# Gates and two key products taken up column by column, and a tile of w_in loaded among the modulation's tiles

## The chip, the core and the metric

One core of a Trainium2 chip runs the whole program. The metric is the device time of one execution in microseconds; of the kernel before, three runs are shown, and their median counts. The engines are TensorE (PE; its weight loads are listed apart as PEld), VectorE (DVE), ScalarE (ACT), GpSimd (POOL) and SyncE (SP), which here issues nearly all DMA transfers. Each engine works through a queue of its own in order, and waits on semaphores for the others.

## The reference

Two transformer blocks run on 256 tokens of 1024 features, in float32. Only the head of the first block matters here:

```python
mod = jnp.matmul(c_act, w_ada[l]) + b_ada[l]
sh_m, sc_m, gt_m, sh_f, sc_f, gt_f = jnp.split(mod, N_MOD, axis=-1)
h = modulate(rmsnorm(x, norm_mix_g[l]), sh_m, sc_m)
proj = jnp.matmul(h, w_in[l])
q, k, v, f_logit, u = jnp.split(proj, split_pts, axis=-1)
log_f = jax.nn.log_sigmoid(f_logit.astype(jnp.float32) + b_fgate[l].astype(jnp.float32))
attn_out = forgetting_attention(q, k, v, log_f)
```

`c_act` is one vector, silu(c), so `mod` is a vector of 6 x 1024. Attention, a pooling branch, a mixture of 32 experts (read whole, 96 MB) and a second block follow. `lb` is a bound of the second block's forget gates, a softmax over two rows of 512 numbers.

## The kernel before

**Stream.** Weights come in tiles of 128 x 2048 numbers (1 MB). `Stream.add` lists them in the order of the string `plan` (line 183) with the slot of a ring that each takes; `a` stands for the modulation's tiles of shift and scale of the first half (8), `b` and `c` for its other two groups, `i` for w_in (8), `o` for w_out (4). SP issues the loads in that order, each when its slot is free and when the load eight places ahead of it has landed. `next()` gives a whole tile. `next2()` gives half a tile of w_in split into an upper part `whi` (line 70, ACT) and a lower part `wlo` (line 71, DVE), with up to two halves split ahead; there are three buffers of each.

**Modulation.** `ada_first` (line 280 on) handles tile d of group a, which holds what column d (features 128 d to 128 d + 127) needs of shift and scale: eight matmuls with the vector `cs` as weights (line 292, 32 rows each), a copy to SBUF by ACT (`mr`, line 294), two matmuls with ones that sum over the partitions (line 298), an addition of the bias into `modT` (line 299). The products of column d + 1 are issued ahead of the sums of column d. Then `A1` (line 359) and `evac_split` (lines 337 to 353) make column d of the modulated input out of the transposed x: an upper part `hT`, a lower part `hL`. Even columns use DVE, ACT, POOL in turn; odd columns ACT, DVE, DVE.

**Products.** `mmx` (lines 140 to 142) takes three matmuls for one product of split operands: upper x upper, upper x lower, lower x upper. When all eight columns stand, PE computes the forget gate `pf` (24 matmuls with 8 columns of weights), then the four key products by `feat` (24 matmuls and a copy to `kT`, line 395, each), the values, and then queries and pooling inputs. The gate's tail (lines 377 to 390: ACT functions, a scan on DVE, a three-way split into `F3`) is needed by the first attention scores. Between products, `some()` takes up a tile of groups b or c: four matmuls on PE (line 311), an accumulation on DVE (lines 313, 315).

**Start.** ACT and DVE make `cs` from c, then `lb` and `olb` (lines 226 to 232), then the row statistics of x (`rms_scale`) and the scaled `xn` (lines 257, 259); PE transposes `xn` in 16 steps (`transposed`, line 274) ahead of everything else.

Of the kernel before, what the change touches and what calls it, by code (L numbers as in the profile page):

```python
# [9 lines left out]
F32 = mybir.dt.float32  # L10
# [4 lines left out]
OP = mybir.AluOpType  # L15
# [8 lines left out]
def nb(tag):  # L24
    return {"f3": 3, "t5": 5}.get(tag, 4)
# [97 lines left out]
def body(tc, nc, ctx, a, out):  # L123
# [56 lines left out]
    st.slots.update({i: (ring if i < 4 else ring2, f"w{i}") for i in range(11)})  # L180

    st.slots.update({15: (hp_, "hT"), 16: (hp_, "hL")})
    plan = "a0-7 0-7 i0-4 0-4 b0-3 5-8 i5 9 b4 10 b5 5 i6 6 b6-7 7-8 c0 0 i7 1 c1-2 2-3 o0 8 c3 10 c4 5 c5 7 o1 0 c6 4 c7 2 o2 3 o3 10"
    src = {"a": (a["w_ada"][0], 0), "b": (a["w_ada"][1], 0), "c": (a["w_ada"][2], 0), "i": (a["w_in"], 1), "o": (a["w_out"], 1)}

    def span(x):
# [31 lines left out]
    G.memset(cs, 0.0)  # L218
    V.tensor_tensor(cs[:, :, 0], cT, ce, op=OP.mult)


    lbl = vec[:, V_LB:V_LB + 8].rearrange("p (r h) -> p r h", r=2)
    lb = cp.tile([128, 4], F32, name="lb")
    olb = cp.tile([128, 4], F32, name="olb")
    le_ = q1.tile([128, 2, 4], F32, name="le_")
    V.tensor_tensor(lb, lbl[:, 0], lbl[:, 1], op=OP.max)
    V.tensor_tensor(le_, lbl, lb[:, None, :].to_broadcast([128, 2, 4]), op=OP.subtract)
    S.activation(le_, le_, AF.Exp)
    V.tensor_tensor(lb, le_[:, 0], le_[:, 1], op=OP.add)
# [34 lines left out]
    for t in range(2):
        scale_rows(xn, xt, r1, t)

    def transposed(ps, tag, src):
        r = []
        for c2 in range(4):
            pt = ps.tile([128, 2, 256], F32, name="ptr", tag=tag, bufs=nb(tag))  # L270
            for c in range(2):
                for t in range(2):
                    d = 2 * c2 + c
                    nc.tensor.transpose(pt[:, c, 128 * t:128 * t + 128], src[:, t, 128 * d:128 * d + 128], ident)
            r += [pt[:, 0], pt[:, 1]]
        return r

    xT = transposed(ps, "a", xn)


    modT = cp.tile([128, 6, 8], F32, name="modT")

    def ada_first():

        last = None
        for d in range(9):
            if d < 8:
                w = st.next()
                pa = ps.tile([128, 512], F32, name="pa", tag="m", bufs=2)
                for k in (0, 2, 4, 6, 1, 3, 5, 7):  # L290
                    j = 32 * (k // 2)
                    mm(pa[j:j + 32, 0:256], cs[:, k, :], w[:, 256 * k:256 * k + 256], start=(k % 2 == 0), stop=(k % 2 == 1))
                mr = q1.tile([128, 256], F32, name="mr", bufs=2)
                S.activation(mr, pa[:, 0:256], AF.Copy)
            if last:
                pl, ml = last
                for j in range(2):
                    mm(pl[:, 256 + j:257 + j], ml[:, 128 * j:128 * j + 128], ones, start=True, stop=True)
                V.tensor_tensor(modT[:, 0:2, d - 1], pl[:, 256:258], vec[:, V_BA + d - 1:V_BA + 16:8], op=OP.add)
                yield  # L300
            last = pa, mr
# [27 lines left out]
    def mod(m):  # L329
        return modT[:, m]  # L330
# [27 lines left out]
    for d, _ in enumerate(ada_first()):
        V.scalar_tensor_tensor(A1[:, d:d + 1], mod(1)[:, d:d + 1], 1.0, vec[:, V_GM + d:V_GM + d + 1], op0=OP.add, op1=OP.mult)
        evac_split(q1, xT[d], hT[:, d], hL[:, d], A1[:, d:d + 1], mod(0)[:, d:d + 1], v=d % 2)  # L360
    st.split_to(LOOK)
# [8 lines left out]
    G.memset(F3, 0.0)  # L370
    catH = q1.tile([128, 8, 256], F32R, name="catH")
    catL = q1.tile([128, 8, 256], F32R, name="catL")

    pf = ps.tile([128, 256], F32, name="pf", tag="a", bufs=4)
    for k in range(8):
        mmx(pf[0:8], (wfh[:, k], wfl[:, k]), (hT[:, k], hL[:, k]), start=(k == 0), stop=(k == 7))
    fz = q1.tile([8, 256], F32, name="fz", tag="mr", bufs=2)
    S.activation(fz, pf[0:8], AF.Identity, bias=vec[0:8, V_BF:V_BF + 1])
    fa = q1.tile([8, 256], F32, name="fa", tag="mr", bufs=2)
    S.activation(fa, fz, AF.Abs)  # L380
    S.activation(fa, fa, AF.Exp, scale=-1.0)
# [9 lines left out]
    def feat(w, dst, scale=1.0):
        p = ps.tile([128, 256], F32, name="pp", tag="a", bufs=4)
        for k in range(8):
            mmx(p, sub(w, slice(None), slice(128 * k, 128 * k + 128)), (hT[:, k], hL[:, k]), start=(k == 0), stop=(k == 7))
        S.activation(dst, p, AF.Copy, scale=scale)
# [1395 lines left out]
```

## Time and profile before

| what | value |
|---|---|
| median of three runs | 743.89 us (743.48 to 747.61) |
| the profiled execution, its own time | 744.4 us |
| its span in the trace | 742.8 us |
| PE busy | 677.4 us (91%) |
| DVE busy | 396.8 us (53%) |
| ACT busy | 303.5 us (41%) |
| DMA, first 350 us | about 420 GB/s, but for two dips |
| DMA, whole span | 207.70 MB, mean 280 GB/s |

Busy time of PE is modelled at its matmuls' ends, and matmuls overlap, so a busy PE is not a PE at its peak. Shares are means over stages with different limits; the prediction reads single stretches.

### The profile page before, as it was taken

How to read it: one execution, taken by the hardware profiler on the slowest of the kernel's cores; microseconds unless marked ns; L12 is line 12 of the kernel's file. 1: busy time of each engine (PE TensorE's matmuls, PEld its weight loads, DVE VectorE, ACT ScalarE, POOL GpSimd, SP SyncE). 2: the span in 40 equal slices, each digit the busy share in tenths (PEclk: the TensorE clock that was granted, in tenths of full speed). 3: DMA queues.
4: the chain of work that ended last, by engine and by line, in shares of the span. 5: the costliest groups of instructions: out<-in, count | busy, mean ns of one | idle time of the engine just before them, and what ended most of it. 6: DMA issues, size and time to landing. Idle time of an engine off the chain costs nothing.

```text
span 742.8 us, 12245 instructions
## 1 busy us (share of the span) xinstructions
PE 677.4 (91%) x4953; PEld 524.9 (71%) x4953; DVE 396.8 (53%) x664; ACT 303.5 (41%) x531; POOL 132.9 (18%) x134
## 2 busy tenths in 40 slices
PE   3899999889799777768999999999999999999995
PEld 2698867654244313132799999999989998989885
DVE  2676896522122102020888876877867654545545
ACT  3644534320011001000675566596456654535433
POOL 0103521000000000000204242212413530503201
PEclk9999999999979979898999999999999999999998
DMA  9999599989999999999764333355446556455411
GB/s 356 419 420 415 205 398 421 419 356 422 420 417 422 421 421 421 421 422 421 301 227 169 116 114 114 115 207 191 170 170 212 214 180 217 170 195 203 171 58 56
DMA packets 29726, 207.70 MB, mean 280 GB/s; under 512 B 3553, under 2 KB 3937, under 8 KB 4706
## 3 DMA queue, kind: packets, MB, share of 16 engines
q1 hardware_dynamic: 29520, 206.35, 70.8%
q8 instruction: 41, 0.67, 0.4%
q10 hardware_dynamic: 146, 0.53, 0.2%
q14 instruction: 19, 0.16, 0.1%
HBM read 205.81 MB, written 1.05 MB: 279 GB/s over the span
## 4 chain that ended last, share of the span: by engine, by line
PE 53%; DMA 15%; DVE 3%; issue 1%; ACT 1%; DVEq 0%; ACTq 0%; SPq 0%
DMA w<-in_w_gu 11%; PE pp L140 9%; PE pp L141 9%; PE pp L142 9%; DMA w<-in_w_dn 4%; PE fy L142 4%; PE fy L141 4%; PE fy L140 4%; PE pB L1274 2%; PE pg L810 2%; PE y L847 2%; PE pv L140 1%; PE pd L964 1%; PE pv L142 1%; PE pv L141 1%; PE acc L141 1%
## 5 line engine op out<-in xcount | busy, mean ns | idle before, releaser
L71 DVE TENSOR_TENSOR wlo<-w,whi 128x1024 fp32r<-128x1024 f32 x146 | 184.7, 1268 | 98.9 <-ACT whi L70 98.8
L70 ACT ACTIVATE whi<-w 128x1024 fp32r<-128x1024 f32 x146 | 153.3, 1054 | 78.3 <-PE fy L142 39.7
L140 PE MATMUL pp<-hT,whi 128*128 128x256 f32 x368 | 104.4, 284 | 0.0
L142 PE MATMUL pp<-hT,wlo 128*128 128x256 f32 x368 | 102.5, 279 | 0.5 <-DVE wlo L71 0.5
L141 PE MATMUL pp<-hL,whi 128*128 128x256 f32 x368 | 102.3, 278 | 0.0
L930 PE MATMUL pgu<-w,hg 128*32 128x512 f32 x512 | 67.7, 646 | 22.6 <-DMA w<-in_w_gu 22.5
L140 PEld LDWEIGHTS pp<-hT,whi 128*128 128x128 f32 x368 | 69.2, 188 | 3.4 <-issue 2.4
L140 PE MATMUL pp<-nH,whi 128*128 128x256 f32 x256 | 71.5, 279 | 0.0
L141 PE MATMUL pp<-nL,whi 128*128 128x256 f32 x256 | 71.3, 279 | 0.0
L142 PE MATMUL pp<-nH,wlo 128*128 128x256 f32 x256 | 71.3, 279 | 0.0
L142 PEld LDWEIGHTS pp<-hT,wlo 128*128 128x128 f32 x368 | 69.2, 188 | 0.8 <-DVE wlo L71 0.7
L141 PEld LDWEIGHTS pp<-hL,whi 128*128 128x128 f32 x368 | 69.4, 189 | 0.0
L930 PEld LDWEIGHTS pgu<-w,hg 128*32 128x32 f32 x512 | 14.2, 112 | 72.5 <-issue 46.3
L1553 POOL TENSOR_TENSOR aL<-rs,aH 128x256 fp32r<-128x256 f32 x32 | 46.2, 1445 | 86.6 <-ACT aH L1552 80.7
L934 DVE TENSOR_TENSOR act<-pgu,act 128x256 f32<-128x256 f32 x8 | 3.4, 424 | 105.3 <-ACT act L933 105.3
L933 ACT ACTIVATE act<-pgu 128x256 f32<-128x256 f32 x8 | 3.1, 384 | 128.2 <-PE pgu L930 128.2
L142 PEld LDWEIGHTS pp<-nH,wlo 128*128 128x128 f32 x256 | 48.6, 190 | 0.0
L141 PE MATMUL fy<-wlo,aH 128*128 128x512 f32 x124 | 48.2, 389 | 0.0
L140 PE MATMUL fy<-whi,aH 128*128 128x512 f32 x124 | 48.2, 389 | 0.0
L142 PE MATMUL fy<-whi,aL 128*128 128x512 f32 x124 | 48.2, 389 | 0.0
L141 PEld LDWEIGHTS pp<-nL,whi 128*128 128x128 f32 x256 | 48.1, 188 | 0.1
L140 PEld LDWEIGHTS pp<-nH,whi 128*128 128x128 f32 x256 | 48.1, 188 | 0.1
(428 smaller groups left out, 1276.1 us busy)
## 6 DMA issues: line engine op xcount, KB each, us to landing
w<-in_w_gu SPq DMA_DIRECT2D x64, 1024.0 KB, 19.6
w<-in_w_dn SPq DMA_DIRECT2D x32, 1024.0 KB, 19.6
w<-in_w_ff SPq DMA_DIRECT2D x32, 1024.0 KB, 4.8
w<-in_w_in SPq DMA_DIRECT2D x30, 1024.0 KB, 5.4
w<-in_w_ada SPq DMA_DIRECT2D x24, 1024.0 KB, 12.9
w<-in_w_out SPq DMA_DIRECT2D x8, 1024.0 KB, 4.7
w<-in_w_o SPq DMA_DIRECT2D x4, 1024.0 KB, 4.8
xt<-in_x SPq DMA_DIRECT2D x1, 1024.0 KB, 5.0
```

Of the source, the lines that this page charges most:

```text
L70: nc.scalar.activation(hi, w, AF.Copy)
L71: low = lambda e, lo=lo, w=w, hi=hi: e.tensor_tensor(lo, w, hi.bitcast(F32), op=OP.subtract)
L140: mm(out_, l[0], r[0], start=start, stop=False)
L141: mm(out_, l[0], r[1], start=False, stop=False)
L142: mm(out_, l[1], r[0], start=False, stop=stop)
L810: mm(pg[:, d], xn[:, t, 512 * b + 128 * d:512 * b + 128 * d + 128], Pf[:, t], start=(t == 0), stop=(t == 1))
L847: mm(pacc[t][h], pw[g][:, 128 * t:128 * t + 128], o, start=False, stop=(g == 7))
L930: mm(pgu[32 * j:32 * j + 32], hg[g][:, k, 32 * j:32 * j + 32], w[:, 512 * j:512 * j + 512], start=(k == 0), stop=(k == 7))
L934: V.tensor_tensor(act, pgu[:, 256:512], act, op=OP.mult)
L964: mm(pd[32 * j:32 * j + 32], aT[:, f, 32 * j:32 * j + 32], w[:, 512 * j:512 * j + 512], start=(f == 0), stop=(f == 1))
L1274: mm(p[:, 4 * t + h], kt[:, h, 128 * t:128 * t + 128], qo[:, h, n * t:n * t + n], start=True, stop=True)
L1553: G.tensor_tensor(aL[:, f], s, aH[:, f].bitcast(F32), op=OP.subtract)
```

## The change

Four things are done.

1. In `plan`, the first tile of w_in (i0) is loaded after four of the modulation's eight tiles, into slot 8 instead of slot 0; tile b3 goes to slot 0 instead of slot 8. The rest of the order stays.
2. `ada_first` is taken apart into `ada_products(d)` and `ada_sums(d)`; the latter also makes column d of `hT` and `hL`. The products of column 0 are issued ahead of the transposes, and the transposes, four at a time (`turned0`), between the first columns.
3. `column(i, ks, kinds)` issues the matmuls of the forget gate (i = 2) and of the first two key products (i = 0, 1) for given columns only. It is called between the modulation's steps, as far as columns stand. Both halves of i0 are split after the sums of column 3. The gate and kT[1] take their PSUM buffers from tag "s". The number of matmuls is as before.
4. kT[2] and kT[3] come next, and only then the gate's tail; `lb` and `olb` are moved from the start to behind the gate's tail.

```diff
-    plan = "a0-7 0-7 i0-4 0-4 b0-3 5-8 i5 9 b4 10 b5 5 i6 6 b6-7 7-8 c0 0 i7 1 c1-2 2-3 o0 8 c3 10 c4 5 c5 7 o1 0 c6 4 c7 2 o2 3 o3 10"
+    plan = "a0-3 0-3 i0 8 a4-7 4-7 i1-4 1-4 b0-2 5-7 b3 0 i5 9 b4 10 b5 5 i6 6 b6-7 7-8 c0 0 i7 1 c1-2 2-3 o0 8 c3 10 c4 5 c5 7 o1 0 c6 4 c7 2 o2 3 o3 10"
...
-    V.tensor_tensor(lb, lbl[:, 0], lbl[:, 1], op=OP.max)
-    V.tensor_tensor(le_, lbl, lb[:, None, :].to_broadcast([128, 2, 4]), op=OP.subtract)
-    S.activation(le_, le_, AF.Exp)
-    V.tensor_tensor(lb, le_[:, 0], le_[:, 1], op=OP.add)
-    V.reciprocal(lb, lb)
-    V.tensor_tensor(lb, lb, le_[:, 0], op=OP.mult)
-    V.tensor_scalar(olb, lb, -1.0, 1.0, op0=OP.mult, op1=OP.add)
...
+    def column(i, ks, kinds=((0, 0), (0, 1), (1, 0))):
+
+        if i == 2 and not pf:
+            pf.append(ps.tile([128, 256], F32, name="pf", tag="s", bufs=2))
+        if i < 2 and not early:
+            early.extend((ps.tile([128, 256], F32, name="pp", tag=tag, bufs=n), st.next2(False)) for tag, n in (("a", 4), ("s", 2)))
+        for m, n in kinds:
+            for k in ks:
+                o, w = (pf[0][0:8], (wfh, wfl)[m][:, k]) if i == 2 else (early[i][0], early[i][1][m][:, 128 * k:128 * k + 128])
+                c = begun[i] = begun.get(i, 0) + 1
+                mm(o, w, (hT, hL)[n][:, k], start=(c == 1), stop=(c == 24))
+
+    upper_, lower_ = ((0, 0), (0, 1)), ((1, 0),)
+    ada_products(0)
+    for t in range(2):
+        scale_rows(xn, xt, r1, t)
+    turned0(0)
+    ada_sums(0)
+    turned0(1)
+    ada_products(1)
+    turned0(2)
+    ada_sums(1)
+    turned0(3)
+    ada_products(2)
+    column(2, (0,))
+    ada_sums(2)
+    column(2, (1,))
+    ada_products(3)
+    ada_sums(3)
+    st.split_to(2)
+    column(2, (2,))
+    column(0, (0, 1, 2), upper_)
+    column(0, (0, 1, 2), lower_)
+    ada_products(4)
+    column(1, (0, 1, 2))
+    for d in range(4, 7):
+        ada_sums(d)
+        ada_products(d + 1)
+        if d < 6:
+            for i in range(3):
+                column(i, (d - 1,))
+    column(0, (5,))
+    column(1, (5,))
+    ada_sums(7)
+    st.split_to(1)
+    column(2, (5,))
+    for i in range(3):
+        column(i, (6,))
+    both = ((0, 0), (1, 0))
+    for i in range(3):
+        column(i, (7,), both)
+    for i in range(3):
+        column(i, (7,), ((0, 1),))
...
+    for i in range(2):
+        S.activation(kT[:, i], early[i][0], AF.Copy)
+    for i in range(2, 4):
+        feat(st.next2(), kT[:, i])
     fz = q1.tile([8, 256], F32, name="fz", tag="mr", bufs=2)
-    S.activation(fz, pf[0:8], AF.Identity, bias=vec[0:8, V_BF:V_BF + 1])
+    S.activation(fz, pf[0][0:8], AF.Identity, bias=vec[0:8, V_BF:V_BF + 1])
...
-    for i in range(4):
-        feat(st.next2(), kT[:, i])
+
+    lbl = vec[:, V_LB:V_LB + 8].rearrange("p (r h) -> p r h", r=2)
+    V.tensor_tensor(lb, lbl[:, 0], lbl[:, 1], op=OP.max)
...
     some(1)
```

**PE, around the middle of the modulation.** In the kernel before, columns 5 to 7 and the start of the gate (`pa` holds a column's products, `pf` the gate, `pp` a key product; x8 are the eight products, x2 the two sums of a column, `w_` and a number a tile of the stream):

```order
L292 MATMUL pa<-w_268,cs 32x256 x8
L298 MATMUL pa<-ones,mr 128x1 x2
L292 MATMUL pa<-w_289,cs 32x256 x8
L298 MATMUL pa<-ones,mr 128x1 x2
L292 MATMUL pa<-w_310,cs 32x256 x8
L298 MATMUL pa<-ones,mr 128x1 x4
L140 MATMUL pf<-hT,wfh 8x256
```

Now, from column 3's products to column 4's:

```order
L276 MATMUL pa<-w_234,cs 32x256 x8
L285 MATMUL pa<-ones,mr 128x1 x2
L358 MATMUL pf<-hT,wfh 8x256
L358 MATMUL pf<-hL,wfh 8x256
L358 MATMUL pf<-hT,wfl 8x256
L358 MATMUL pp<-hT,whi 128x256 x3
L358 MATMUL pp<-hL,whi 128x256 x3
L358 MATMUL pp<-hT,wlo 128x256 x3
L276 MATMUL pa<-w_279,cs 32x256 x8
```

Between the sums of column 3 and the products of column 4 stand three matmuls of the gate and nine of kT[0], which need the split i0; PE takes nothing from behind them before they have run.

**ACT, around the gate's tail.** Before, from the last column's evacuation on (`whi` is an upper half, w_339, w_396 and w_521 are i0, i1 and i3; `fz` and `fa` are the gate's tail):

```order
L344 ACTIVATE evt<-ptr,modT,A_168 128x256
L70 ACTIVATE whi<-w_339 128x1024 x2
L378 ACTIVATE fz<-pf,vec 8x256
L380 ACTIVATE fa<-fz 8x256
L381 ACTIVATE fa<-fa 8x256
L382 ACTIVATE fa<-fa,ones 8x256
L70 ACTIVATE whi<-w_396 128x1024
L395 ACTIVATE kT<-pp 128x256
L70 ACTIVATE whi<-w_396 128x1024
```

Now, with w_437 for i2 and the exponential of lb as `le__120`:

```order
L417 ACTIVATE kT<-pp 128x256
L70 ACTIVATE whi<-w_437 128x1024
L417 ACTIVATE kT<-pp 128x256
L430 ACTIVATE fz<-pf,vec 8x256
L432 ACTIVATE fa<-fz 8x256
L433 ACTIVATE fa<-fa 8x256
L434 ACTIVATE fa<-fa,ones 8x256
L447 ACTIVATE le__120<-le__120 128x8
L70 ACTIVATE whi<-w_521 128x1024 x2
```

The gate's tail has moved from ahead of i1's first upper half to behind kT[3]'s copy, and i3's upper halves (the third value product) stand behind it and behind lb's exponential.

**DVE, ahead of the first accumulation of group b.** Before (`F_353` is F3, w_525 is b0, w_562 b1):

```order
L387 CAST F_353<-fF 8x256
L71 TENSOR_TENSOR wlo<-w_396,whi 128x1024 x2
L71 TENSOR_TENSOR wlo<-w_458,whi 128x1024 x2
L315 TENSOR_SCALAR xn<-w_525,cs 128x4x256
L71 TENSOR_TENSOR wlo<-w_521,whi 128x1024
L313 SCALAR_TENSOR_TENSOR xn<-w_562,cs,xn 128x4x256
L71 TENSOR_TENSOR wlo<-w_521,whi 128x1024
```

Now (the first row is the gate's last):

```order
L439 CAST F_427<-fF 8x256
L445 TENSOR_TENSOR lb<-vec 128x4
L446 TENSOR_TENSOR le__120<-vec,lb 128x8
L448 TENSOR_TENSOR lb<-le__120 128x4
L449 RECIPROCAL lb<-lb 128x4
L450 TENSOR_TENSOR lb<-lb,le__120 128x4
L451 TENSOR_SCALAR olb<-lb 128x4
L302 TENSOR_SCALAR xn<-w_525,cs 128x4x256
L71 TENSOR_TENSOR wlo<-w_521,whi 128x1024
```

Six steps of lb, and the gate's seven in front of them, now stand between i2's lower halves and the accumulation of b0, and i3's first lower half behind that.

## Rows read from the trace of the kernel before

**Rows 1.** page, busy tenths in 40 slices, the DMA line

```profile
DMA  9999599989999999999764333355446556455411
```

**Rows 2.** busy time by stretch; last columns PEclk, DMA share, GB/s

```profile
12.00:15.40 3.40, 3.39 (x16) 3.01 (x17) 0.28 (x2) 0.35 (x1) 0.00 (x0) 1.00 1.02 431
...
33.00:60.00 27.00, 26.50 (x233) 24.00 (x232) 18.70 (x21) 13.04 (x22) 0.00 (x0) 1.00 1.01 419
```

**Rows 3.** timeline, issues on SP's queue and ACT's

```profile
57.82 0.85 SPq L51 DMA_DIRECT2D w<-in_w_ada  x2
...
82.67 0.33 SPq L51 DMA_DIRECT2D w<-in_w_out  x1
...
152.68 0.51 ACTq L841 DMA_DIRECT2D grow<-in_gain  x1
```

**Rows 4.** timeline from 7 us, DVE, ACT, PE: start, us, what, [idle before]

```profile
7.23 0.15 DVE L226 TENSOR_TENSOR lb<-vec 128x4 f32<-128x4 f32 x1
...
7.62 0.21 ACT L228 ACTIVATE le__120<-le__120 128x8 f32<-128x8 f32 x1 [1.31 <-DVE le__120 L227]
...
7.74 1.04 ACT L251 ACTIVATE xn<-xt 128x1024 f32<-128x1024 f32 x1
...
8.47 0.17 DVE L232 TENSOR_SCALAR olb<-lb 128x4 f32<-128x4 f32 x1
...
11.20 1.15 ACT L259 ACTIVATE xn<-xt,r 128x1024 f32<-128x1024 f32 x1 [0.62 <-DVE r L245]
...
12.01 3.46 PE L274 MATMUL ptr<-ident,xn 128*128 128x128 f32 x16 [12.01 <-DVE xn L257]
```

**Rows 5.** two lines' weight loads: min/median/max ns, starts

```profile
L274 PEld LDWEIGHTS ptr<-ident,xn x16: 140/230/230, 12.0 to 15.1; 128*128 128x128 f32 x16
...
L865 PEld LDWEIGHTS ptr<-ident,xt x32: 137/141/143, 354.7 to 560.3; 128*128 128x128 f32 x32
```

**Rows 6.** timeline, a column on PE, an odd column's evacuation

```profile
18.20 1.07 PE L292 MATMUL pa<-w,cs 128*32 128x256 f32 x16 [0.32 <-DVE modT L299]
...
19.19 0.52 PEld L298 LDWEIGHTS pa<-ones,mr 128*128 128x128 f32 x4 [0.41 <-issue]
...
20.30 0.56 ACT L344 ACTIVATE evt<-ptr,modT,A 128x256 f32<-128x256 f32 x1 [0.52 <-DVE A L359]
```

**Rows 7.** timeline, ACT, upper halves of i0

```profile
31.30 1.99 ACT L70 ACTIVATE whi<-w 128x1024 fp32r<-128x1024 f32 x2
```

**Rows 8.** timeline, ACT, DVE, PE, forget gate and keys

```profile
33.24 0.46 ACT L378 ACTIVATE fz<-pf,vec 8x256 f32<-8x256 f32 x1
...
36.70 0.38 ACT L395 ACTIVATE kT<-pp 128x256 f32<-128x256 f32 x1 [0.61 <-PE pp L142]
...
39.42 0.38 ACT L395 ACTIVATE kT<-pp 128x256 f32<-128x256 f32 x1 [1.39 <-PE pp L142]
...
38.26 2.36 DVE L71 TENSOR_TENSOR wlo<-w,whi 128x1024 fp32r<-128x1024 f32 x2
...
39.54 0.39 PE L142 MATMUL pp<-hT,wlo 128*128 128x256 f32 x1
```

**Rows 9.** timeline, issues of a and b tiles, uses of b0, b2

```profile
2.82 4.84 SPq L51 DMA_DIRECT2D w<-in_w_ada  x8
...
27.75 4.00 SPq L51 DMA_DIRECT2D w<-in_w_ada  x4
...
44.86 0.75 DVE L315 TENSOR_SCALAR xn<-w,cs 128x1024 f32<-128x1024 f32 x1
...
44.96 0.64 PE L311 MATMUL pa<-w,cs 128*32 128x256 f32 x8
...
52.15 0.64 PE L311 MATMUL pa<-w,cs 128*32 128x256 f32 x8
```

**Rows 10.** DMA issues, a0 and b0 (last column: us to landing)

```profile
w<-in_w_ada SPq DMA_DIRECT2D x1, 1024.0 KB, 6.5
...
w<-in_w_ada SPq DMA_DIRECT2D x1, 1024.0 KB, 15.9
```

More of the change, by code (lines that the diff above doesn't have):

```diff
@@ L219, in body @@
     V.tensor_tensor(cs[:, :, 0], cT, ce, op=OP.mult)
-    lbl = vec[:, V_LB:V_LB + 8].rearrange("p (r h) -> p r h", r=2)
     lb = cp.tile([128, 4], F32, name="lb")
@@ L263, in body @@
     rms_scale(r1, xt, q1, xn)
[L264 to L276, printed above, removed]
@@ L278, in body @@
-    xT = transposed(ps, "a", xn)
-    modT = cp.tile([128, 6, 8], F32, name="modT")
[L283 to L301, printed above, removed]
+    xT = []
@@ new lines, in turned0, with ada_products @@
+    def turned0(c2):
+        pt = ps.tile([128, 2, 256], F32, name="ptr", tag="a", bufs=4)
+        for c in range(2):
+            for t in range(2):
+                d = 2 * c2 + c
+                nc.tensor.transpose(pt[:, c, 128 * t:128 * t + 128], xn[:, t, 128 * d:128 * d + 128], ident)
+        xT.extend([pt[:, 0], pt[:, 1]])
+    modT = cp.tile([128, 6, 8], F32, name="modT")
+    pas = {}
+    def ada_products(d):
+        w = st.next()
+        pa = ps.tile([128, 512], F32, name="pa", tag="m", bufs=2)
+        for k in (0, 2, 4, 6, 1, 3, 5, 7):
+            j = 32 * (k // 2)
+            mm(pa[j:j + 32, 0:256], cs[:, k, :], w[:, 256 * k:256 * k + 256], start=(k % 2 == 0), stop=(k % 2 == 1))
+        mr = q1.tile([128, 256], F32, name="mr", bufs=2)
+        S.activation(mr, pa[:, 0:256], AF.Copy)
+        pas[d] = pa, mr
@@ new lines, in ada_sums @@
+    def ada_sums(d):
+        pl, ml = pas.pop(d)
+        for j in range(2):
+            mm(pl[:, 256 + j:257 + j], ml[:, 128 * j:128 * j + 128], ones, start=True, stop=True)
+        V.tensor_tensor(modT[:, 0:2, d], pl[:, 256:258], vec[:, V_BA + d:V_BA + 16:8], op=OP.add)
+        V.scalar_tensor_tensor(A1[:, d:d + 1], mod(1)[:, d:d + 1], 1.0, vec[:, V_GM + d:V_GM + d + 1], op0=OP.add, op1=OP.mult)
+        evac_split(q1, xT[d], hT[:, d], hL[:, d], A1[:, d:d + 1], mod(0)[:, d:d + 1], v=d % 2)
@@ L357, in body @@
     hL = hp_.tile([128, 8, 256], F32R, name="hL", tag="hL")
[L358 to L361, printed above, removed]
+    pf, early, begun = [], [], {}
+    def column(i, ks, kinds=((0, 0), (0, 1), (1, 0))):
[10 more added lines that the diff above has]
+    ada_products(0)
+    for t in range(2):
+        scale_rows(xn, xt, r1, t)
[36 more added lines that the diff above has]
+        column(i, (7,), ((0, 1),))
     nc.sync.dma_start(wpl, a["w_pool"])
@@ L372, in body, with feat, some @@
     catL = q1.tile([128, 8, 256], F32R, name="catL")
-    pf = ps.tile([128, 256], F32, name="pf", tag="a", bufs=4)
-    for k in range(8):
-        mmx(pf[0:8], (wfh[:, k], wfl[:, k]), (hT[:, k], hL[:, k]), start=(k == 0), stop=(k == 7))
+    def feat(w, dst, scale=1.0):
+        p = ps.tile([128, 256], F32, name="pp", tag="a", bufs=4)
+        for k in range(8):
+            mmx(p, sub(w, slice(None), slice(128 * k, 128 * k + 128)), (hT[:, k], hL[:, k]), start=(k == 0), stop=(k == 7))
+        S.activation(dst, p, AF.Copy, scale=scale)
+    adas = chain(ada_next(1), ada_next(2))
+    def some(n):
+        for _ in range(n):
+            next(adas, None)
+    for i in range(2):
+        S.activation(kT[:, i], early[i][0], AF.Copy)
+    for i in range(2, 4):
+        feat(st.next2(), kT[:, i])
     fz = q1.tile([8, 256], F32, name="fz", tag="mr", bufs=2)
-    S.activation(fz, pf[0:8], AF.Identity, bias=vec[0:8, V_BF:V_BF + 1])
+    S.activation(fz, pf[0][0:8], AF.Identity, bias=vec[0:8, V_BF:V_BF + 1])
     fa = q1.tile([8, 256], F32, name="fa", tag="mr", bufs=2)
@@ L389, in body @@
             V.tensor_tensor(fF, fF, F3[32 * i:32 * i + 8], op=OP.subtract)
[L391 to L395, printed above, removed]
-    adas = chain(ada_next(1), ada_next(2))
-    def some(n):
-        for _ in range(n):
-            next(adas, None)
-    for i in range(4):
-        feat(st.next2(), kT[:, i])
+    lbl = vec[:, V_LB:V_LB + 8].rearrange("p (r h) -> p r h", r=2)
+    V.tensor_tensor(lb, lbl[:, 0], lbl[:, 1], op=OP.max)
+    V.tensor_tensor(le_, lbl, lb[:, None, :].to_broadcast([128, 2, 4]), op=OP.subtract)
+    S.activation(le_, le_, AF.Exp)
+    V.tensor_tensor(lb, le_[:, 0], le_[:, 1], op=OP.add)
+    V.reciprocal(lb, lb)
+    V.tensor_tensor(lb, lb, le_[:, 0], op=OP.mult)
+    V.tensor_scalar(olb, lb, -1.0, 1.0, op0=OP.mult, op1=OP.add)
     some(1)
```

## The prediction

> **What bounds the kernel now.** I read the page's forty slices first. The transfer line stays at 9 until about 352 us, with two dips, in the fifth slice (74 to 93 us) and the ninth (149 to 167 us) [rows 1]. Reading the weights therefore sets the pace of the first 350 us, except where the stream has nothing to fetch into. Next come the queues [rows 3]. SP hands out the last second-group tiles at 57.82, and the next one (w_out, slot 8) only at 82.67, 24 us later, when the tile in that slot has been used up. The second dip ends with a small transfer on ACT's queue at 152.68, which stands behind the router's arithmetic. So both dips end when computation gets far enough, not when a transfer lands. Time gained or lost by the engines ahead of 82 us moves w_out, the router, and from there the whole stream by as much. Then the stages: from 33 to 60 us PE is busy 26.5 of 27 us [rows 2], so there a PE delay is a delay of everything. Ahead of 33 us lies the stretch that the change rewrites, and there PE has gaps. I call the eight first modulation tiles a0 to a7, the tiles of w_in i0 to i7, the next modulation tiles b0 to b7.
>
> **The stretch before.** PE starts its transposes at 12.01 and its last key matmul of the second product (kT[1]) near 39.1, 0.3 ahead of that product's copy at 39.42 [rows 4, 8]. In between stand 16 transposes (3.46 us with the wait for ACT and the last one's tail, [rows 4]; 0.2 each), eight groups of column products (18.20 to 19.19 with the switch, 0.98 each), eight column sums (0.52 each [rows 6]), 72 matmuls for forget gate, kT[0] and kT[1]. Those cost 0.113 each: the copies at 36.70 and 39.42 lie 24 matmuls apart [rows 8]. The sum is 3.4 + 7.8 + 4.2 + 8.2 = 23.6 us of the 27.1: PE stands still for 3.5 us. More than that cannot be won.
>
> **The change, part by part.**
>
> *lb leaves the start.* Its exponential at 7.62 had ACT idle for 1.31 us, waiting for DVE, and the square of x starts behind it at 7.74 [rows 4]. Without it ACT goes on at 6.31, and the row statistics come 1.4 us earlier: DVE and ACT could scale x at 9.8 instead of 11.2.
>
> *First products ahead of the transposes.* a0 lands at 2.82 + 6.5 = 9.3 [rows 9, 10]. The eight products start there. Their price is not in the trace, for PE is slow at its start, as the rows show: the first transposes load weights in 230 ns, the same shape takes 141 later [rows 5], though the granted clock of this stretch reads 1.00 [rows 2]. I bound the group by 0.98 and 0.98 x 230/141 = 1.6 us and take 1.6, since it is now the first work of the engine. It ends at 10.9. ACT must copy the result (0.38, a copy of the size of those in [rows 8]) before it scales the second half of x (1.15, [rows 4]), because the copy now stands ahead in its queue: 11.0 + 0.4 + 1.15 gives 12.65 for the second transpose, where it was 12.4 before. The 1.4 us are spent.
>
> *Work from there.* 15 transposes 3.05, seven groups 6.9, eight sums 4.2, 72 matmuls 8.2: 22.35, so 35.0 if PE never waits.
>
> *Waits in the new order.* Sums of columns 2 and 3 now follow their own products almost at once, and wait for the copy (0.25 and 0.8, the second behind a cast of column 2 on ACT). The split of i0 stands in ACT's queue behind column 3's evacuation. An odd column's evacuation starts 1.1 us after its sums (19.19 to 20.30) and takes 0.56 [rows 6]; then comes one upper half, 1.0 [rows 7]. By my walk the sums start at 21.95, the half is ready at 24.7, and PE is there at 22.8: 1.9 us. The lower half follows 1.2 later [rows 8] and costs 0.55 more. Smaller waits for columns 5 and 7 and for the last hT add 0.8. Together 4.3 us, more than the 3.5 that stood there before. The last early matmul is at 39.3, where it was 39.1.
>
> *The next product, kT[2].* In the kernel before its third matmul ran at 39.54 [rows 8], its weights having been split while PE worked. Now the split of i1's first half stands behind column 7's evacuation: upper half 37.8 to 38.85, lower half to 40.05. kT[2] passes there at 40.1. **First term: +0.5 us**, and kT[3] ends that much later than 44.96.
>
> *Forget gate and lb behind kT[3].* Before, the gate's tail ran at 33.24 to 38.22 on ACT and DVE, beside kT[0] and kT[1] [rows 8]. Now it stands behind kT[3]'s copy, lb behind the gate, b0's accumulation behind lb, and the split for the third value product behind them all. From the end of kT[3]: copy 0.58 with its hand-over, gate 33.24 to 38.26 = 5.0, lb 7.23 to 8.64 = 1.4 [rows 4], accumulation 0.75 [rows 9], lower half 1.2 [rows 8]: 8.9 us. PE asks for that lower half after two value products and three b products. Before, from b0's product at 44.96 to b2's at 52.15 and past it, that was 8.05 us [rows 9]. **Second term: +0.85 us.** DVE needs some 10 us to work off its queue, but the next lower halves are then due later than they are ready.
>
> *The plan and the loads.* The same bytes precede b0, so it lands at 27.75 + 15.9 = 43.65 as before [rows 9, 10]. From a0 at 9.3 to b0 stand 13 tiles and two small loads, so a tile takes 2.56 us; a7, now eight tiles behind a0, lands at 29.8, and PE reaches it at 33.9 by my walk: nothing. Slot 8 is free early, b7 gains, c0 waits for b3 instead: nothing, since c0 stands ten tiles behind b0 and lands near 69 at the earliest. b0's slot is given back some 8 us later, so b5 is issued near 53; the stream may pause a microsecond, ahead of a dip of some nine.
>
> **Sum:** 0.5 + 0.85 = +1.4 us (rounded up). The profiled execution took 744.4, so 745.8 by it; that execution lies 0.5 above the median of 743.9, and against the median I say **745.3 us**. This is 0.2%, and about 0.5% (3.7 us) is what a measurement of this kernel can tell from no change.
>
> **A rule against the row.** Rows 5 show slow first transposes, and I let them stay slow (0.2 each) from 12.65 on. The Trainium skill, "TensorE: Matmul & The Clock Gate", Part 1, says that the default state of the engine's clock is throttled and that activity releases it. The trace agrees in so far as the fastest of these transposes, unlike their median, load in 140 ns. By that rule the products at 9.3 would already have released it, and the result is the first rival below.
>
> **Rivals.**
>
> 1. *PE is at full pace by 12.65.* Fifteen transposes at 0.2 x 141/230 = 0.12 save 1.2 us: +0.5 - 1.2 + 0.85 = +0.1, 744.0. For it: 1.6 us of work before. Against it: a pause of about 1.5 us follows, and before, more than half of sixteen transposes in a row stayed at 230. Chance 0.22.
> 2. *The gaps close (the other side).* If i0's halves are ready when PE reaches the first key column, and the copies come in time, kT[3] ends near 41 (44.96 + 0.5 - 4.3). It decides at that first key column: a wait under half a microsecond there speaks for it. Then b0's landing at 43.65 bounds the rest, 1.3 us ahead of its use at 44.96 before; and the lower half of the third value product is ready in time, since the gate began earlier. -1.3: 742.6. Chance 0.15.
> 3. *The gate's tail is hidden.* If DVE passes b0 and lb faster than I add up, or PE comes later, only the first term stays: 744.4. The same holds if part of the loss is taken up between 60 and 150 us, where PE and DVE wait for each other. Chance 0.13.
> 4. *PE stays slow longer,* since its early work is spread thin: sums and products of columns 0 and 1 at 230/141 add 0.95, and a second late lower half up to 0.9: +3.3, 747.2. Chance 0.07.
> 5. The change does something outside these sums; 0.03.
>
> **How the numbers follow.** My forecast, both terms with their roundings (744.5 to 746.2), has 0.40. Range: from rival 2's bound, 742.6, to rival 4's, 747.2; about 2 in 10 lie outside once noise of half a microsecond is allowed for at the ends. All named cases lie within 3.7 us of 743.9: within 0.5% 0.93, slower by more 0.05 (part of rival 4 and of 5), faster by more 0.02.
>
> **What would show it.** Right: the first transposes near 11 and 12.6; a PE wait of 1 to 2 us for whi ahead of the first early key matmul; kT[2]'s third matmul near 40.1, waiting for wlo; a PE wait near 53 for the wlo of the third value product; b0's accumulation on DVE near 52 instead of 44.86; w_out issued near 84 instead of 82.67. Wrong: kT[2] under way before 38.5, or PE waiting for b0 itself; then the time falls below 743.9. A w_out issue that moves by another amount than the end would mean that the later stages do not pass a shift on.

## The result, and the profile after

The changed kernel took **749.62 us** in the median, the kernel before 744.13 us beside it: ratio 1.0063, 95% interval 1.0052 to 1.0074. That is slower by 4.7 us by the ratio (5.5 between the medians), outside the range that ended at 747.2, and on the side to which the prediction gave 0.05. The profiled execution of after took 749.62 us (span 748.0, 5.2 more than before's).

PE's timeline of after follows; columns: start, us, engine, line, operation, tiles, count and, in brackets, the idle time before it and what ended it.

```profile
9.31 1.94 PE L276 MATMUL pa<-w,cs 128*32 128x256 f32 x16 [9.31 <-DVE isu L234]
...
12.78 0.90 PE L262 MATMUL ptr<-ident,xn 128*128 128x128 f32 x3 [1.12 <-ACT xn L250]
...
15.21 1.94 PE L276 MATMUL pa<-w,cs 128*32 128x256 f32 x16
...
19.21 1.07 PE L276 MATMUL pa<-w,cs 128*32 128x256 f32 x16
...
23.39 0.61 PE L285 MATMUL pa<-ones,mr 128*128 128x1 f32 x4 [0.56 <-ACT mr L278]
...
24.09 0.28 PE L358 MATMUL pf<-hT,wfl 128*8 128x256 f32 x1
26.12 1.01 PE L358 MATMUL pp<-hT,whi 128*128 128x256 f32 x3 [1.75 <-ACT whi L70]
...
28.33 1.94 PE L276 MATMUL pa<-w,cs 128*32 128x256 f32 x16
...
32.70 1.07 PE L276 MATMUL pa<-w,cs 128*32 128x256 f32 x16
...
43.83 0.39 PE L142 MATMUL pp<-hT,wlo 128*128 128x256 f32 x1 [0.32 <-DVE wlo L71]
...
49.26 0.64 PE L298 MATMUL pa<-w,cs 128*32 128x256 f32 x8
...
56.44 0.64 PE L298 MATMUL pa<-w,cs 128*32 128x256 f32 x8
...
57.87 0.38 PE L141 MATMUL pv<-wlo,hT 128*128 128x256 f32 x1 [0.48 <-DVE wlo L71]
...
60.78 0.64 PE L298 MATMUL pa<-w,cs 128*32 128x256 f32 x8
```

Read the group of eight products (L276, sixteen records) as a ruler: it takes 1.07 at full pace and 1.94 at half. It reads 1.94 at 9.31 and 15.21, 1.07 from 19.21, and **1.94 again at 28.33**, behind the wait for the upper half of i0. kT[2]'s third matmul stands at 43.83, 4.29 later than in [rows 8], and b0's product at 49.26, 4.30 later than in [rows 9]. From b2's to b3's product pass 4.34 us; the last early wait is the 0.48 for the third value product's lower half.

Busy time by stretch in after, on PE, PEld, DVE, ACT and POOL; the last three columns are granted clock, DMA share and GB/s.

```profile
15.00:18.00 3.00, 3.00 (x23) 1.52 (x22) 0.37 (x1) 0.80 (x2) 0.73 (x1) 1.00 1.01 426
...
22.00:24.00 2.00, 1.44 (x22) 0.84 (x15) 0.49 (x1) 0.80 (x2) 0.72 (x1) 1.00 1.01 422
24.00:26.00 2.00, 0.37 (x3) 0.07 (x1) 1.04 (x4) 1.45 (x3) 0.00 (x0) 0.85 1.01 410
26.00:28.00 2.00, 1.88 (x9) 1.89 (x9) 1.90 (x2) 1.02 (x2) 0.00 (x0) 0.50 1.02 426
28.00:30.00 2.00, 2.00 (x18) 0.70 (x17) 0.46 (x1) 0.00 (x0) 0.00 (x0) 0.50 0.99 414
30.00:32.00 2.00, 2.00 (x12) 1.80 (x9) 0.00 (x0) 0.38 (x1) 0.00 (x0) 0.50 1.06 412
32.00:34.00 2.00, 2.00 (x25) 1.40 (x24) 0.86 (x3) 0.15 (x1) 0.00 (x0) 0.94 1.03 428
```

PE was busy for 0.37 of 2 us from 24 to 26; then the granted clock stands at 0.50 (1.2 GHz) for more than six microseconds, in which PE hardly rests, and returns to 1.00 (2.4 GHz). In the kernel before it read 1.00 there; two rows of before:

```profile
24.00:26.00 2.00, 1.74 (x24) 1.01 (x28) 1.14 (x6) 0.95 (x2) 0.00 (x0) 1.00 1.00 406
...
30.00:32.00 2.00, 2.00 (x19) 1.49 (x18) 1.27 (x4) 1.49 (x3) 1.00 (x4) 1.00 1.02 422
```

The row of 15:18 in after also shows what the column leaves out: it reads 1.00, as in every stretch up to 24 us, although the groups at 9.31 and 15.21 are slow.

Later rows of after, from the queues of SP and ACT (answering to [rows 3]; the first is b5's issue), then DVE's timeline around the accumulation of b0 (L302; [rows 9] had it at 44.86).

```profile
56.76 0.33 SPq L51 DMA_DIRECT2D w<-in_w_ada  x1
...
87.70 0.33 SPq L51 DMA_DIRECT2D w<-in_w_out  x1
...
155.76 0.51 ACTq L889 DMA_DIRECT2D grow<-in_gain  x1
```

```profile
54.62 0.16 DVE L445 TENSOR_TENSOR lb<-vec 128x4 f32<-128x4 f32 x1
...
55.94 0.74 DVE L302 TENSOR_SCALAR xn<-w,cs 128x1024 f32<-128x1024 f32 x1
56.60 1.22 DVE L71 TENSOR_TENSOR wlo<-w,whi 128x1024 fp32r<-128x1024 f32 x1
```

w_out is issued 5.03 later, the small transfer on ACT's queue 3.08 later, the span ends 5.2 later.

### The profile page after: what moved, and what is told of

Read it like the earlier page. It is cut to its first block, busy times and chain, and to the rows that moved or that the text cites. A ratio compares the mean times of both kernels' runs of the same rounds, so it can differ in the third digit from the quotient of the medians.

```text
span 748.0 us, 12238 instructions
## 1 busy us (share of the span) xinstructions
PE 680.9 (91%) x4953; PEld 526.8 (70%) x4953; DVE 395.8 (53%) x664; ACT 302.7 (40%) x531; POOL 133.5 (18%) x134
## 3 DMA queue, kind: packets, MB, share of 16 engines
HBM read 205.81 MB, written 1.05 MB: 277 GB/s over the span
## 4 chain that ended last, share of the span: by engine, by line
PE 50%; DMA 18%; DVE 2%; issue 1%; ACT 1%; DVEq 0%; SPq 0%; ACTq 0%
DMA w<-in_w_gu 11%; PE pp L140 9%; PE pp L142 9%; PE pp L141 9%; DMA w<-in_w_dn 7%; PE fy L141 4%; PE fy L142 4%; PE fy L140 4%; PE pB L1322 2%; PE pv L140 1%; PE pv L142 1%; PE pv L141 1%; PE y L895 1%; PE acc L141 1%; PE acc L140 1%; PE acc L142 1%
## 5 line engine op out<-in xcount | busy, mean ns | idle before, releaser
L140 PE MATMUL pp<-hT,whi 128*128 128x256 f32 x352 | 100.0, 284 | 0.0
L142 PE MATMUL pp<-hT,wlo 128*128 128x256 f32 x352 | 98.0, 278 | 0.3 <-DVE wlo L71 0.3
L141 PE MATMUL pp<-hL,whi 128*128 128x256 f32 x352 | 97.8, 278 | 0.0
L140 PEld LDWEIGHTS pp<-hT,whi 128*128 128x128 f32 x352 | 66.2, 188 | 3.4 <-issue 2.4
L142 PEld LDWEIGHTS pp<-hT,wlo 128*128 128x128 f32 x352 | 66.2, 188 | 0.5 <-DVE wlo L71 0.5
L141 PEld LDWEIGHTS pp<-hL,whi 128*128 128x128 f32 x352 | 66.4, 189 | 0.0
```

## The experiments

All twelve were run with repetitions beside the kernel before on the same chip (its median there: 744.3 to 744.6); e5 to e8 ran on another chip than the other eight. Each trace is of a single execution, and its time can lie off the version's median: by 1.8 to 2.5 us below it in e1, e5, e10 and e11, 2.4 above it in e8. So the traces are read for places, and the medians for times. The theories: **A**, PE's pace: the unforeseen part of the loss is work at half pace, at the start and behind the wait. **B**, the waits and the order of the queues make it, and pace only fills time that would be waited.

In code, `column(0, ())` only takes the first two keys' PSUM tiles and weights; e1 to e12 below are the names' first parts.

### Busy through the wait

```
+    column(0, ())
+    for _ in range(16):
+        mm(early[0][0], hT[:, 0, 0:128], hT[:, 0], start=True, stop=True)
     column(0, (0, 1, 2), upper_)
```

> The kernel after with 16 products of 128x256 added ahead of the first key column, whose results are overwritten; PE is busy with them while it waits for the upper half of i0's first column. Theory A (pace): the loss is PE at half pace between 26 and 32.3 us, because its granted clock fell in the wait; kept busy, it stays at 1.00 there, the key columns 0 and 1 and products(4) take half as long, b0's first product stands near 46.5 instead of 49.26, and the time is near 747.0 (2.6 below after's 749.6). Theory B (waits): the loss is the sum of the waits for halves and copies, and PE's pace only fills time that it would wait; b0's product stays at 49.3 or moves later, time 749.6 to 750.3.

Ratio to before 1.0038 (1.0017 to 1.0058), median 747.48. First PE's timeline, then busy time by stretch:

```profile
24.28 2.07 PE L381 MATMUL pp<-hT 128*128 128x256 f32 x16
26.20 0.63 PE L358 MATMUL pp<-hT,whi 128*128 128x256 f32 x3
...
28.01 1.07 PE L276 MATMUL pa<-w,cs 128*32 128x256 f32 x16
...
30.57 1.07 PE L276 MATMUL pa<-w,cs 128*32 128x256 f32 x16
...
47.13 0.64 PE L298 MATMUL pa<-w,cs 128*32 128x256 f32 x8
```

```profile
24.00:26.00 2.00, 2.00 (x19) 1.94 (x18) 1.04 (x4) 1.37 (x2) 0.00 (x0) 1.00 1.02 414
26.00:28.00 2.00, 1.71 (x12) 1.33 (x11) 1.82 (x2) 1.09 (x2) 0.00 (x0) 1.00 1.00 418
28.00:30.00 2.00, 2.00 (x25) 1.41 (x25) 0.54 (x1) 0.39 (x1) 0.00 (x0) 1.00 1.01 422
```

This is the experiment that tells A from B. The first key column starts where it did (26.20, was 26.12), since its half comes no earlier. But the clock stays at 1.00 and the products of column 4 take 1.07: b0's product stands at 47.13, **2.13 us earlier**, by added work whose result is thrown away. A had said 46.5, B 49.3. The time says the same: A's 747.0 lies in the interval, B's 749.6 to 750.3 beyond it (748.9).

### The half of i0 split earlier

```
     ada_products(3)
+    st.split_to(1)
     ada_sums(3)
     st.split_to(2)
```

> The kernel after with the first half of i0 split ahead of column 3's sums and evacuation instead of behind them. The upper half is ready near 24.4 and the lower near 25.6, when PE asks for them at 24.2 and 24.9. Theory A (pace): the wait of 1.75 shrinks under 0.5, the granted clock stays at 1.00 from 24 to 32, b0's product stands near 45.5 to 46.5, time 746.0 to 747.0. Theory B (waits): only the wait itself is saved, 1.0 to 1.5 us, so b0 near 48 and 748.3. If the clock falls all the same with the short waits, the fall is older than this wait, and the time stays within 1 us of after's.

Ratio 1.0005 (0.9985 to 1.0024), median 745.15: nearly all of the loss is back. PE's timeline:

```profile
24.20 0.62 PE L358 MATMUL pp<-hT,whi 128*128 128x256 f32 x3
...
25.46 0.62 PE L358 MATMUL pp<-hT,wlo 128*128 128x256 f32 x3 [0.29 <-DVE wlo L71]
...
46.04 0.64 PE L298 MATMUL pa<-w,cs 128*32 128x256 f32 x8
```

One line saves the wait of 1.75 and, with it, the half pace: three waits are left from 24 to 32 us (0.29, 0.25, 0.29), and the granted clock reads 1.00 in every stretch there. A's number for b0's product held (46.04), and the time came out below A's 746.0 to 747.0; B's 48 did not hold.

### The gate's tail and lb ahead of the keys

```
+    fz = q1.tile([8, 256], F32, name="fz", tag="mr", bufs=2)
...
+    V.tensor_scalar(olb, lb, -1.0, 1.0, op0=OP.mult, op1=OP.add)
     for i in range(2):
         S.activation(kT[:, i], early[i][0], AF.Copy)
     for i in range(2, 4):
         feat(st.next2(), kT[:, i])
-    fz = q1.tile([8, 256], F32, name="fz", tag="mr", bufs=2)
...
-    V.tensor_scalar(olb, lb, -1.0, 1.0, op0=OP.mult, op1=OP.add)
```

> The kernel after with the gate's tail and lb put back ahead of the copies of kT[0] and kT[1], where the gate stood before. Theory of the prediction's second term: the wait of PE for the lower half at 57.87 goes, w_out's issue comes 0.7 earlier than after's 87.70, time near 748.9. Rival: the gate's tail now stands in the queues of ACT and DVE ahead of the splits for kT[2] and kT[3], these products wait for their weights by 1 to 3 us, and the time rises to 750 to 752.

Ratio 1.0144 (1.0116 to 1.0172), median 755.67: the rival, and worse than it said. PE's timeline:

```profile
49.48 0.58 PE L140 MATMUL pp<-hT,whi 128*128 128x256 f32 x1 [3.81 <-ACT whi L70]
...
55.34 0.64 PE L298 MATMUL pa<-w,cs 128*32 128x256 f32 x8
```

ACT waits for DVE's half of the gate and lb until 47.73, and only then copies the keys and splits. PE waits 3.81 us, the granted clock falls to 0.50 from 48 to 54, and b0's product comes at 55.34. So the gate's place behind kT[3] is not what made the change slow; in this order it is needed.

### All transposes first

```
-    ada_products(0)
     for t in range(2):
         scale_rows(xn, xt, r1, t)
-    turned0(0)
+    for c2 in range(4):
+        turned0(c2)
+    ada_products(0)
     ada_sums(0)
-    turned0(1)
     ada_products(1)
-    turned0(2)
     ada_sums(1)
-    turned0(3)
     ada_products(2)
```

> The kernel after with all 16 transposes ahead of the first column products, as before, and lb still behind kT[3]. Theory A (pace) with the start: the slow stretch until 18.6 costs about 1 us, and transposes in one piece bring PE to full pace by 15; products(3) then end up to 1 us earlier, but the wait for the upper half of i0 only grows by as much, since the split waits for ACT's own queue: 749 to 750 unless column 3's evacuation comes earlier too. Theory B: the first products at 9.3 were filling idle time, so putting them behind the transposes delays all column sums by about 1.5 us: 751.

Ratio 1.0061 (1.0042 to 1.008), median 750.14, b0's product at 49.03 (after: 49.26). PE reaches full pace earlier here, as A had it (the group at 16.65 takes 1.07), but it starts its first work later (10.72) and waits 0.51 and 0.82 for ACT's copies. So the column products ahead of the transposes neither win nor lose; the wait for i0's half is again 1.75, at 25.98, and the clock falls again. B's 751 lies just beyond the interval (750.5), and b0's product speaks against it too.

### lb behind the value products

Beside the earlier split (lb's seven instructions, the first and the last shown):

```
-    V.tensor_tensor(lb, lbl[:, 0], lbl[:, 1], op=OP.max)
...
-    V.tensor_scalar(olb, lb, -1.0, 1.0, op0=OP.mult, op1=OP.add)
     some(1)
...
             S.activation(vt[:, t, 256 * i:256 * i + 256], pv[t], AF.Copy)
+    V.tensor_tensor(lb, lbl[:, 0], lbl[:, 1], op=OP.max)
...
+    V.tensor_scalar(olb, lb, -1.0, 1.0, op0=OP.mult, op1=OP.add)
```

> The kernel e2_split_early with lb's seven instructions moved from ahead of b0's accumulation to behind the value products. Theory of the second term: PE's wait of 0.48 for the lower half of the third value product (54.66 in e2) goes and the distance from b2's to b3's product falls from 4.35 to 3.6, so w_out is issued 0.7 earlier than in e2 (84.50) and the time falls by 0.7 to near 744.4. Rival: the wait comes from the gate's tail and the accumulation alone, or the 0.7 is taken up before 84 us by another wait; then w_out and the time stay within 0.2 of e2's.

Ratio 1.0015 (0.9999 to 1.0031), median 745.57. The time can't tell (the intervals overlap); PE's timeline can:

```profile
52.88 0.64 PE L298 MATMUL pa<-w,cs 128*32 128x256 f32 x8
...
56.47 0.64 PE L298 MATMUL pa<-w,cs 128*32 128x256 f32 x8
```

The wait is gone, 3.59 us pass from b2's to b3's product instead of 4.35, and w_out is issued at 83.43: 1.07 earlier, of which 0.35 come from an earlier b0. The second term is 0.7 us, and lb's 1.4 us on DVE and ACT are enough to make it.

### lb's place alone, in both kernels

In the kernel before:

```
     le_ = q1.tile([128, 2, 4], F32, name="le_")
-    V.tensor_tensor(lb, lbl[:, 0], lbl[:, 1], op=OP.max)
...
             S.activation(vt[:, t, 256 * i:256 * i + 256], pv[t], AF.Copy)
+    V.tensor_tensor(lb, lbl[:, 0], lbl[:, 1], op=OP.max)
...
```

> The kernel before with lb's seven instructions moved from the start to behind the value products: one part of the change, alone. The transposes start near 10.7 instead of 12.01. Theory: in the kernel before, the column products follow the landings (the last waited for its tile, 27.82), so the 1.3 us are taken up there, products(7) stays at 27.8 and the time at 744.1 to 744.6. Rival: the start passes its 1.3 us on, the key products and w_out come earlier, 743.

It became slower: 1.0024 (1.0011 to 1.0038), median 746.42. Neither the theory nor its rival expected that. PE's transposes started at 10.59 (was 12.01), products(7) stood at 27.66 (27.82), as the theory said. But then:

```profile
30.00:31.00 1.00, 1.00 (x8) 0.61 (x6) 0.55 (x3) 0.65 (x2) 0.15 (x1) 0.54 1.06 439
31.00:32.00 1.00, 1.00 (x6) 0.65 (x5) 0.72 (x1) 1.00 (x2) 0.93 (x4) 0.50 0.99 410
```

(busy time by stretch, columns as above). The clock fell in the forget gate's matmuls, and b0's product came at 46.28 instead of 44.96. None of PE's waits from 24 to 30 us was over 0.32 here. Why it fell in this execution and not in the profile of before, whose waits there are as short (0.26 to 0.43), isn't shown.

In the kernel after:

```
     le_ = q1.tile([128, 2, 4], F32, name="le_")
+    V.tensor_tensor(lb, lbl[:, 0], lbl[:, 1], op=OP.max)
...
-    V.tensor_tensor(lb, lbl[:, 0], lbl[:, 1], op=OP.max)
...
     some(1)
```

> The kernel after with lb's seven instructions put back at the start, where they stood before. Theory: in the changed order the early work is one chain from the row statistics over copies and evacuations to the split of i0, so the 1.3 us come back at the start (transposes near 12.5 and 14), the first key column starts near 27.2, PE's half pace stays, the second term's 0.73 goes: near 750.2. Rival: the start is hidden behind the waits of column 3; then only the second term's 0.73 is won and the time is 748.9.

This gave 1.0046 (1.0026 to 1.0066), median 748.71. The trace holds what the theory said: the first key column at 27.11 (expected 27.2), b0's product at 50.01 (0.75 later than after's), then 3.59 instead of 4.34 from b2 to b3, so that w_out's issue, 87.75, is after's 87.70. The time sides with the rival: its 748.9 lies in the interval (746.3 to 749.3), the theory's 750.2 beyond it. The trace is of the slowest of seven executions (751.07), and the half pace lasted for a shorter while in it than in after: from the first key column to products(5) pass 5.92 us, in after 6.58. So by the places lb's move costs about 1 us at the first key column and wins 0.75 at the value products; what it is worth in time isn't settled.

### PE busy before the first tile lands

```
+    warm = ps.tile([128, 256], F32, name="warm", tag="s", bufs=2)
+    for _ in range(32):
+        mm(warm[:, 0:128], ident, ident, start=True, stop=True)
     ada_products(0)
```

> The kernel e5_lb_late with 32 products of ident by ident (128x128, results unused) ahead of products(0), from about 1.6 us on, so that PE has worked when a0 lands. Theory A (pace): products(0) take 1.07 instead of 1.94, the transposes' weight loads read 141 instead of 230 ns, and the first key column comes 1 to 2 us earlier than in e5; b0's product moves from 46.0 to 44.5 and the time falls by 1 to 1.5. Rival: the order of ACT (mr copies, second half of x, evacuations) sets the first 25 us and PE's pace there is hidden: within 0.4 of e5.

The same with fewer:

```
-    for _ in range(32):
+    for _ in range(26):
```

> The kernel e7_warm with 26 instead of 32 warming products, so that they end near 9.3, when a0 is there, instead of 10.6. If what counts is that PE has worked before, products(0) start 1.2 earlier at 1.07 and b0's product comes up to 1 us earlier than e7's 44.29, with 43.65 (b0's landing before) as its floor: time 742.3 to 743.0. Rival: 26 are too few and the transposes are slow again (230 ns loads); then b0's product goes back to 45 or more and the time to 744.

On top of the earlier split and the late lb: 0.9976 (0.9965 to 0.9987), median 742.98, with 32 products; 0.9973 (0.9959 to 0.9987), median 742.86, with 26. PE's timeline, and then the weight loads of the sixteen transposes (minimum, median, maximum in ns; [rows 5] had 140/230/230), with 32:

```profile
1.58 9.10 PE L363 MATMUL warm<-ident 128*128 128x128 f32 x64 [1.58 <-DVE ident L158]
10.61 1.07 PE L276 MATMUL pa<-w,cs 128*32 128x256 f32 x16
...
44.29 0.64 PE L298 MATMUL pa<-w,cs 128*32 128x256 f32 x8
```

```profile
L262 PEld LDWEIGHTS ptr<-ident,xn x16: 138/140/223, 11.6 to 16.8; 128*128 128x128 f32 x16
```

The first real products start 1.1 later than in the kernel without (9.49) and still everything behind them is earlier: b0's product at 44.29 instead of 45.69. The median fell by 2.6, b0's product by 1.4 (A had 1 to 1.5 for the time; e5's median lay 2.2 above its own profiled execution). With 26 they start at 10.27 and b0's product stands at 43.95.

> The kernel after with the 32 warming products and nothing else. Theory A: the start's half pace goes (1.4 us), but the wait for i0's upper half stays at 1.75, and with it the fall of the granted clock behind it: 748 to 748.5, 1.00 until 24 and 0.5 behind. If the fall at 26 needed a PE that had been slow before, it stays away here: b0's product near 45.7 and 745.5.

These are the 32 products in **after**, with nothing else changed: 1.0040 (1.0023 to 1.0056), median 747.73. PE's timeline, then busy time by stretch:

```profile
24.09 0.62 PE L358 MATMUL pp<-hT,whi 128*128 128x256 f32 x3 [1.75 <-ACT whi L70]
...
46.76 0.64 PE L298 MATMUL pa<-w,cs 128*32 128x256 f32 x8
```

```profile
24.00:26.00 2.00, 1.62 (x9) 1.18 (x9) 1.93 (x2) 0.99 (x2) 0.00 (x0) 0.93 1.04 434
26.00:28.00 2.00, 2.00 (x18) 0.73 (x17) 0.43 (x1) 0.00 (x0) 0.00 (x0) 0.50 0.99 414
28.00:30.00 2.00, 2.00 (x13) 2.00 (x13) 0.00 (x0) 0.39 (x1) 0.00 (x0) 0.72 1.03 430
```

The first key column comes 2.03 us earlier (26.12 in after), the wait is 1.75 as ever, and the clock falls behind it all the same, for a shorter while: from 24.09 to products(5) at 30.03 pass 5.94 us, in after 6.58, in e1 4.37. So a start at full pace does not keep the second loss away.

In the kernel before:

```
+    warm = ps.tile([128, 256], F32, name="warm", tag="s", bufs=2)
+    for _ in range(36):
+        mm(warm[:, 0:128], ident, ident, start=True, stop=True)
     xT = transposed(ps, "a", xn)
```

> The kernel before with 36 warming products ahead of its transposes, from 1.6 to about 11.5 us. Theory: in the kernel before, the column products wait for their tiles' landings (27.82), so a faster start only lengthens these waits; b0's product stays near 44.96, the time at 744.1 to 744.6, and what e7_warm gains belongs to the changed order. Rival: the 16 transposes and the first two groups at full pace bring kT[1] 1 to 1.5 us earlier there too, 743.

There the warm start wins nothing: 1.0013 (0.9995 to 1.0032), median 746.09. The transposes take 2.25 instead of 3.46, but PE then waits 0.83 and 0.89 for its tiles, the granted clock falls to 0.50 at 30 to 32, and b0's product stands at 46.01. The theory's reason (the landings set the pace there) held; that b0 would stay at 44.96 did not.

### The scaling of x first

```
+    for t in range(2):
+        scale_rows(xn, xt, r1, t)
     ada_products(0)
-    for t in range(2):
-        scale_rows(xn, xt, r1, t)
```

> The kernel e9_warm_short with the scaling of x ahead of products(0)'s copy in ACT's queue. The second half of x is ready near 11.1 instead of 12.8, PE's wait of 1.28 ahead of the second transpose falls under 0.8, and the first copy ends 0.3 later. Theory: one chain over ACT sets the first 23 us, so the key columns start 0.5 to 1.0 earlier than in e9 and the time falls by as much, unless b0's landing (43.65) is then waited for. Rival: the sums of column 0 wait for the later copy and its evacuation shifts everything back: within 0.3 of e9.

Ratio **0.9965** (0.9948 to 0.9981), median 742.13: the fastest version here, 2.3 us below the kernel before (744.48), and 7.5 below after. PE's timeline:

```profile
21.27 0.62 PE L358 MATMUL pp<-hT,whi 128*128 128x256 f32 x3 [0.72 <-ACT whi L70]
...
43.70 0.64 PE L298 MATMUL pa<-w,cs 128*32 128x256 f32 x8 [0.51 <-DMA w<-in_w_ada]
```

PE now waits 0.51 us for b0's tile. In this trace the landing bounds the stretch, so a PE that were earlier still would only wait longer there. The key columns start 0.66 earlier than in e9 (21.93), as expected; that the time is lower than e9's is not clear of noise, for the two intervals overlap.

## Why the prediction was wrong

**The direction and most places were right.** A PE wait of 1 to 2 us for the upper half (1.75, forecast 1.9), kT[2]'s third matmul waiting for its lower half (0.32 of wait), the wait for the third value product's lower half (0.48), b0's accumulation far behind its product: all are in the trace.

**The second term was right.** Forecast 0.85, measured 4.34 - 3.60 = 0.74 between b2's and b3's product; e5 and e8 remove it by moving lb alone. Most of it is the wait of 0.48 inside the third value product. b3's product in before, where b2's stood at 52.15 [rows 9]:

```profile
55.75 0.64 PE L311 MATMUL pa<-w,cs 128*32 128x256 f32 x8
```

**The plan and the loads cost nothing, as forecast.** b5 was issued at 56.76 instead of near 53, and the stream paused for longer than the microsecond of the forecast (66 and 57 GB/s from 54 to 58 us), ahead of the dip. a7 cost PE no wait. w_out moved by 5.03, and 4.30 at b0's product and 0.74 behind it are all of that.

**The first term failed: +4.3 instead of +0.5.** The step that failed is "Work from there", together with the price of the wait for i0 in "Waits in the new order". Of the 22.35 us behind 12.65 only the transposes stood at a slow price; the groups, the sums and the 72 matmuls stood at full pace. And the wait for i0 was priced by its length alone. Two things were missing:

- *At the start.* From 12.78 (forecast 12.65) to the end of its work ahead of the wait at 24.37, PE worked 11.0 us with 0.56 of waits. I had 9.1 with 1.05, to 22.8. The products of column 1 took 1.94, the sums of columns 0 and 1 0.85 and 0.79 (0.50 to 0.61 at full pace). This put the first key column at 26.12 instead of 24.7: 1.4 us. e11 shows what the slow start is worth in whole, with the slow transposes that I had counted: 2.03.
- *Behind the wait.* Key columns 0 and 1, products(4) and the sums of column 4 took 6.58 us, from 26.12 to 32.70, where the filled version (e1) took 4.37 (26.20 to 30.57): 2.2 us. A wait of 1.75 cost 1.75 plus 2.2. This has no line in the prediction. The price is not the same each time: behind the same wait the stretch took 6.49 in e4, and 5.92 to 5.94, 1.6 more than filled, in e3, e8 and e11.

0.5 + 1.4 + 2.2 = 4.1 of the 4.30 measured at b0's product; 0.2 stay without a name.

**The rivals.** The fourth (PE slow longer) had the mechanism's first half, and its price for columns 0 and 1, 0.95, was too small; it let the pace return for good. The first (full pace by 12.65) did not happen: behind one group of products, in after, the transposes load weights in 226 ns in the median, and in e7, where PE had worked from 1.58 on, in 140. The Trainium skill, "TensorE: Matmul & The Clock Gate", Part 1, says that activity releases the throttle. The traces agree for e7's nine microseconds of work, and not yet for after's one group. The second (the gaps close, b0's landing bounds the rest) did not happen in the change, but it is what e12 is: its place, b0's landing, and its sign were right, and 742.1 lies near its 742.6. That is a different kernel, so it is no credit to the forecast; and PE still waits 0.72 for i0's half there, where the rival asked for less than half a microsecond.

**The end.** I said that a w_out issue that moves by another amount than the end would mean that later stages don't pass a shift on. It moved by 5.03, ACT's small transfer by 3.08 and the end by 5.2. Here are two stretches by granted clock, of the profiles of before and of after, in that order:

```profile
148.00:152.00 4.00, 4.00 (x23) 4.00 (x23) 1.51 (x5) 0.00 (x0) 0.00 (x0) 0.57 1.00 416
```

```profile
164.00:168.00 4.00, 3.05 (x14) 2.84 (x15) 0.76 (x2) 0.00 (x0) 0.00 (x0) 0.67 1.00 412
```

Before's profiled execution lost some 2 us at 148 to 152, and after's as much from 164 on (an estimate, from the shifts here), each behind a lightly loaded stretch (PE busy for 2.07 of the 4 us from 144, 2.72 from 160). Such a stretch alone doesn't decide: after has 2.07 from 148 and e2 2.26 from 160, and no fall follows. e2's profile has neither fall: w_out 1.83 later than before's, the small transfer 0.13 earlier, the span 742.9 against 742.8. So these profiles agree with stages that pass a shift on and falls of the clock that come on top, elsewhere in each. I did not try to keep the clock up there.

## What to carry to other kernels

Price a wait of PE by what comes behind it too: look at the granted clock of the stretch and at a group of known length on both sides of the wait. Where work is spread thinner, so that a dense stretch becomes a sparse one with a wait at its end, the saved gaps can be paid back at half pace. A split or copy that a wait hangs on can often be issued one step earlier in its own queue (one line here, 4 us); useless matmuls through the wait or ahead of the first landing are the test of whether pace is the cause, and sometimes the cure.

## What the runs showed of the hardware that I had not expected

- A wait of 1.75 us was followed by some 3.4 to 6.8 us at half clock (worked out from stretches of 2 us) in after, e3, e4, e8 and e11, whether PE had been slow (after) or at full pace (e11) before it. Filled with work, it was not (e1). Waits of 0.25 to 0.72 in e2 and e12 were not followed by a fall in this stretch, but in e6 the clock fell behind waits of at most 0.32, and in e10 behind waits of 0.83 and 0.89; the length of the wait alone doesn't decide.
- The granted clock reads 1.00 from 9 to 18 us in after while the same group takes 1.94, and 1.07 from 19 us on. Durations of a known group are the safer reading at the start.
- Falls elsewhere in the program are not the same in every kernel: in the profiles of e4 and e8 the clock fell from 116 on as well (0.50 from 118 to 120), in those of before, after and e2 it did not.
